# Delta rule on one Trainium2 core: the triangular mask on the query products alone, and the decay exponentials in a buffer of their own

## The chip, the cores and the metric

The kernel runs on one core of a Trainium2 chip. The metric is the device time of one execution in microseconds (us); lower is better. The time before is the median of three runs. The profile is of one further execution, which has a time of its own, and sums are made against that one. The engines are named as in the profile: PE is the matrix engine (PEld its weight loads), DVE the vector engine, ACT the engine of activation functions, POOL the general engine, SP the engine that issues most transfers.

## What is computed

One layer of a hybrid encoder serves two groups of tokens with shared weights: a prompt of 512 tokens and a sample of 64. Its first half is a gated delta rule of 4 heads, each 128 wide, beside a differential attention; then follow an attention over a memory and a feed-forward block. The change touches the delta rule alone. Cut to what matters, its reference is:

```python
G = jnp.cumsum(gc, axis=-1)
diff = G[..., :, None] - G[..., None, :]
gam = jnp.where(tril, jnp.exp(jnp.where(tril, diff, 0.0)), 0.0)
kk = jnp.einsum('nbhid,nbhjd->nbhij', kc, kc)
a_sys = jnp.where(strict, bc[..., :, None] * kk * gam, 0.0) + jnp.eye(C)
u = triangular_solve(a_sys, bc[..., None] * vc, ...)
w = triangular_solve(a_sys, (bc * jnp.exp(G))[..., None] * kc, ...)
qk = jnp.einsum('nbhid,nbhjd->nbhij', qc, kc) * gam
qg = qc * jnp.exp(G)[..., None]

def step(S, xs):
    vn = u_c - w_c @ S
    o = qg_c @ S + qk_c @ vn
    S = S * gl_c + kd_c.T @ vn
```

So the decay factors `gam` enter twice: into the system that is solved (strictly triangular) and into the products of queries and keys (triangular). The plain exponentials `exp(G)` scale keys and queries where they meet the running state `S`.

## The kernel before, in words

The activations lie transposed, features on partitions, and most of the work is projections: 128 output columns at a time are loaded from the weights by SP (L148, L153), split into a high and a low part by ACT and DVE (L157, L158), and multiplied on PE in three products that add up in a bank of PSUM (`project`, L165). In the profile these matmuls are `pr<-u,wh` and `pr<-u,wl`.

The delta rule works on five chunks: four of 128 prompt tokens (c = 0 to 3) and one of 64 sample tokens (c = 4). `gdn_prep` (L566) makes what a chunk needs without the state, and `gdn_scan` (L683) carries the state `S` through it. The program order is prep 0, prep 1, the projection of the gate z, scan 0, prep 2, scan 1, prep 3, scan 2, prep 4, scan 3, scan 4. The time in which each engine takes its instructions is not written out by hand here: a planner with a model of costs orders each engine's queue at compile time, by readiness and program order, and it mixes the projections in between. On the chip each engine then takes its queue strictly in that order and waits by semaphores. So a change of dependencies can also change the order of unrelated instructions.

In `gdn_prep`, in order: keys and queries are turned (L576, L584), squared and summed for their norms (L580 to L588), and POOL takes the reciprocal roots (`rpow`, L204, called at L589). The cumulated decay is spread over rows by PE into the bank `bg` (L596). DVE subtracts (L599) into the buffer `Y`, ACT takes the exponential (L602), and POOL multiplies by the triangular mask `triu` (L603): this is `gam`. PE makes the products of keys (L606), DVE multiplies them with `gam` and a factor into `At` (L609). PE makes the products of keys and queries (L614), DVE multiplies them with `gam` into `KQ` (L616). The values are turned (L623) and scaled into `vb` (L625). For c > 0 ACT takes the exponential of `bg` into the buffer `eg` (L628), and POOL multiplies keys and queries by it (L629, L630). Then the inverse of the system is built up by doubling: `masked` (L632) picks from `At` the entries of one level by the table `lev`, whose lower triangle is zero (L541), into a buffer `B`; PE, ACT and DVE alternate (L643 to L679) until the inverse is `X`.

Two kinds of buffers matter. The banks of PSUM named g0 and g1 belong to even and odd chunks and there is one of each, so that all products of one chunk's prep pass through one bank, each after the readers of the one before. The SBUF buffers `B0` and `B1` have two copies each, and `sq`, `eg` and `B` of a chunk share them. The buffer `aT` has two copies too and is used by the two attentions later (L861, L1000).

`gdn_scan` ends with a norm of its output: ACT squares (L718), DVE sums (L719 to L721), POOL takes the root (L722, in the profile L204), DVE scales (L723, L724). Beside the delta rule the memory is normed at L516: ACT squares (L222), DVE and POOL take the root (L227, L204), DVE scales (L232), PE turns it.

Of the kernel before, what the change touches and what calls it, by code (L numbers as in the profile page):

```python
# [10 lines left out]
AF = mybir.ActivationFunctionType  # L11
ALU = mybir.AluOpType
# [22 lines left out]
def hybrid_layer_kernel(  # L35
# [10 lines left out]
    V, A, G = nc.vector, nc.scalar, nc.gpsimd  # L46
# [28 lines left out]
    def nm(s):  # L75
        uid[0] += 1
        return f"{s}_{uid[0]}"
# [10 lines left out]
    def small(tag, shape, bufs=None):  # L88
        tag = SHARED.get(tag, tag)
        bufs = 1 if tag in ("vn", "on", "S") or tag[:-1] in ("At", "Dt", "Y") else 2  # L90
        return sp.tile(shape, F32, tag=tag, name=nm(tag), bufs=bufs)

    def tiny(shape, tag="tiny", bufs=16):
        return tp.tile(shape, F32, tag=tag, name=nm(tag), bufs=bufs)

    def bank(tag="ba"):
        return ps.tile([P, 512], F32, tag=tag, name=nm(tag), bufs=BANKS[tag])

    def const(shape, name, dt=F32):
        return cp.tile(shape, dt, tag=name, name=name)  # L100
# [40 lines left out]
    triu = const([P, P], "triu")  # L141
# [259 lines left out]
    for typ in (1, 0, 2):  # L401
        cT[typ] = (e5[:, 1], e2[:, 1], e2[:, 0])[typ]
        for h in range(H):
# [7 lines left out]
            n = SOFF + DEC  # L411
# [135 lines left out]
    def v4(ap, n):  # L547
        return ap.rearrange("p (h n) -> p h n", h=4)[:, :, :n]

    def sb(tag, bufs=2):  # L550
        return small(tag, [P, 4, P], bufs)
# [14 lines left out]
    def gdn_prep(c, c0, n):  # L566
        L = slice(c0, c0 + n)

        def st(tag):
            return sb(dict(gam="Y", sq="B", eg="B").get(tag, tag) + str(c % 2))  # L570

        r8 = tiny([P, 8], "tg")
        s8 = tiny([P, 8], "tg")
# [3 lines left out]
        kd = sb("kd")  # L577
        V.tensor_tensor(kd[:n], v4(bk, P)[:n], kdc[:n, c, :].unsqueeze(2).to_broadcast([n, 4, P]), ALU.mult)
        sq = st("sq")
        A.activation(sq[:n], v4(bk, P)[:n], AF.Square)  # L580
        V.tensor_reduce(s8[:n, 0:4], sq[:n], AX.X, ALU.add)
        bq = bank(f"g{c % 2}")
        for h in range(H):
            tr(bq[:n, h * P : (h + 1) * P], cq[:, h, L])  # L584
        sq2 = st("sq")
        A.activation(sq2[:n], v4(bq, P)[:n], AF.Square)
        V.tensor_reduce(s8[:n, 4:8], sq2[:n], AX.X, ALU.add)
# [6 lines left out]
        bg = bank(f"g{c % 2}")  # L594
        for h in range(H):
            mm(bg[:, h * P : h * P + n], bc(gg[:n, c, h : h + 1], [n, P]), triu[:n, :n])  # L596
        gam = st("gam")
        for h in range(H):
            V.tensor_scalar(  # L599
                gam[:n, h, :n], bg[:n, h * P : h * P + n], Gc[:n, c, h : h + 1], 0.0, ALU.subtract, ALU.min  # L600
            )
        A.activation(gam[:n, :, :n], gam[:n, :, :n], AF.Exp)  # L602
        G.tensor_tensor(gam[:n, :, :n], gam[:n, :, :n], triu[:n, :n].unsqueeze(1).to_broadcast([n, 4, n]), ALU.mult)  # L603
        bkk = bank(f"g{c % 2}")
        for h in range(H):
            mm(bkk[:n, h * P : h * P + n], ck[:, h, L], ck[:, h, L])  # L606
# [7 lines left out]
            mm(bkq[:n, h * P : h * P + n], ck[:, h, L], cq[:, h, L])  # L614
        KQ = sb("KQ")
        V.tensor_tensor(KQ[:n, :, :n], v4(bkq, n)[:n], gam[:n, :, :n], ALU.mult)  # L616
        nk, rq2 = tiny([P, 4], "tg"), tiny([P, 4], "tg")
        V.tensor_tensor(nk[:n], s8[:n, 0:4], r8[:n, 0:4], ALU.mult)
        V.tensor_scalar(r8[:n, 4:8], r8[:n, 4:8], P ** -0.5, None, ALU.mult)
# [4 lines left out]
        vb = sb("vb")  # L624
        V.tensor_tensor(vb[:n], v4(bv, P)[:n], nk[:n].unsqueeze(2).to_broadcast([n, 4, P]), ALU.mult)  # L625
        if c > 0:
            eg = st("eg")
            A.activation(eg[:, :, :n], v4(bg, n), AF.Exp)  # L628
            G.tensor_tensor(ck[:, :, L], ck[:, :, L], eg[:, :, :n], ALU.mult)  # L629
            G.tensor_tensor(cq[:, :, L], cq[:, :, L], eg[:, :, :n], ALU.mult)  # L630

        def masked(lv):  # L632
            B = st("B")
            V.scalar_tensor_tensor(  # L634
                B[:n, :, :n], lev[:n, :n].unsqueeze(1).to_broadcast([n, 4, n]), float(lv), At[:n, :, :n],
                ALU.is_equal, ALU.mult,
            )
            return B
# [3 lines left out]
        B = masked(1)  # L642
# [6 lines left out]
        while lv < n:  # L649
            Y = st("Y")  # L650
            by = bank(f"g{c % 2}")
            if lv < 64:
                B = masked(lv)
# [76 lines left out]

    S = None
    prepared = [gdn_prep(*chunks[0][:2], chunks[0][3])]
    for c, c0, t0, n in chunks:
        if c < 4:
            prepared.append(gdn_prep(*chunks[c + 1][:2], chunks[c + 1][3]))
        else:
            nc.sync.dma_start(o_gdn_p[0, 0].rearrange("h k v -> k h v"), S)
            S = sb("S")
            nc.sync.dma_start(S, state_gdn[0, 0].rearrange("h k v -> k h v"))
        if c == 0:  # L740
            project_z()
        S = gdn_scan(c, c0, t0, n, prepared[c], S)
# [256 lines left out]
    for h in range(H):  # L999
# [14 lines left out]
        for t, (q0, _) in enumerate(QT):  # L1014
            t0, n = TT[t]
# [181 lines left out]
```

## Time and profile before

| what | us |
|---|---|
| median of 3 runs (lowest to highest) | 1063.34 (1062.84 to 1063.38) |
| the profiled execution, its own time | 1061.57 |
| its span, first to last instruction | 1059.5 |
| PE busy of the span | 1034.8 |
| DVE, ACT, POOL busy | 671.5, 432.6, 73.8 |

All times in the traces count from the span's start. A row of the timeline gives start, duration, engine, line, operation and `out<-in`, and, in brackets, the idle time of that engine just before and what ended it. A row of windows gives, for a stretch, its length, the busy time of PE, PEld, DVE, ACT and POOL with the number of instructions, the granted PE clock as a share of full speed, the share of the transfer engines and GB/s. Since the three products of a projection are the bulk of the work, PE is busy nearly always; a busy PE can still run at half its clock, which the column of the clock shows.

### The profile page before, as it was taken

What the parts mean: (1) busy time and instruction counts of PE and PEld (TensorE: products, weight loads), DVE (VectorE), ACT (ScalarE), POOL (GpSimd) and SP (SyncE); (2) the same over time, 40 slices, a digit from 0 to 9 for tenths busy, and PEclk for the clock granted to TensorE, in tenths of its full rate; (3) what the DMA queues carried; (4) which work ended last, traced back from release to release, by engine and by line L of the source; (5) the groups of instructions that cost most, each with busy time, mean ns of one, the idle gap of its engine ahead of it and who ended that gap; (6) DMA issues with size and microseconds to landing.
All of it is one profiled execution on the core that took longest, in us unless ns stands there. A gap on an engine that the chain in (4) does not pass through costs nothing.

```text
span 1059.5 us, 16941 instructions
## 1 busy us (share of the span) xinstructions
PE 1034.8 (98%) x6574; PEld 929.9 (88%) x6574; DVE 671.5 (63%) x1471; ACT 432.6 (41%) x897; POOL 73.8 (7%) x126
## 2 busy tenths in 40 slices
PE   8999899999999999999999999999999999999997
PEld 6999898898788877999887799999999999999996
DVE  6767684756467575564555666666666666666674
ACT  6644754333265665343333443323232323222344
POOL 4411120311000000000000000000000000000000
PEclk9999999999999999999999999999999999999998
DMA  7332310100132255524211122132414141323312
GB/s 212 116 120 78 114 41 21 42 1 22 54 88 63 89 179 198 166 80 140 60 41 40 57 83 63 58 100 60 116 47 124 44 119 50 110 59 109 91 51 90
DMA packets 139442, 89.96 MB, mean 85 GB/s; under 512 B 5522, under 2 KB 130576, under 8 KB 138852
## 3 DMA queue, kind: packets, MB, share of 16 engines
q1 hardware_dynamic: 138996, 88.24, 28.0%
q8 instruction: 52, 0.85, 0.3%
q10 hardware_dynamic: 368, 0.66, 0.2%
q14 instruction: 26, 0.21, 0.1%
HBM read 79.14 MB, written 9.74 MB: 84 GB/s over the span
## 4 chain that ended last, share of the span: by engine, by line
PE 90%; issue 4%; DVE 2%; ACT 2%; POOL 1%; DMA 0%; POOLq 0%; ACTq 0%; DVEq 0%
PE pr L103 70%; PE g L103 10%; PE gs L103 3%; PE ba L109 3%; PE ba L103 2%; PE g L109 2%; POOL tg L204 1%; POOL tiny L204 0%; PE pr L109 0%; PE gs L109 0%; ACT wh L157 0%; ACT u L1109 0%; ACT Y L656 0%; POOL u L630 0%; DVE on L724 0%
## 5 line engine op out<-in xcount | busy, mean ns | idle before, releaser
L103 PE MATMUL pr<-u,wh 128*128 128x512 f32 (+1 forms) x2664 | 699.5, 343 | 1.2 <-DVE u L288 0.9
L103 PEld LDWEIGHTS pr<-u,wh 128*128 128x128 f32 x2664 | 456.5, 188 | 37.8 <-issue 1.7
L103 PE MATMUL pr<-u,wl 128*128 128x256 f32 (+1 forms) x1776 | 484.7, 299 | 0.0
L103 PEld LDWEIGHTS pr<-u,wl 128*128 128x128 f32 x1776 | 328.4, 189 | 8.0 <-DVE wl L355 0.3
L157 ACT CAST wh<-raw 128x1024 fp32r<-128x1024 f32 (+1 forms) x153 | 136.5, 892 | 231.2 <-PE pr L103 212.4
L158 DVE TENSOR_TENSOR wl<-raw,wh 128x1024 fp32r<-128x1024 f32 (+1 forms) x153 | 157.4, 1029 | 61.3 <-ACT wh L157 59.5
L943 DVE TENSOR_TENSOR u<-u,pr 128x256 f32<-128x256 f32 (+1 forms) x160 | 72.3, 452 | 62.8 <-PE pr L103 60.2
L204 POOL TENSOR_TENSOR tiny<-tiny,nhalf 128x1 f32<-128x1 f32 (+4 forms) x11 | 10.1, 918 | 664.1 <-DVE tiny L1127 409.3
L197 ACT CAST u<-p 128x256 fp32r<-128x256 f32 x64 | 27.8, 435 | 51.8 <-DVE p L1064 51.8
L103 PE MATMUL pr<-wh,u 128*128 128x512 f32 x128 | 42.6, 405 | 0.0
L198 DVE TENSOR_TENSOR u<-p,u 128x256 fp32r<-128x256 f32 x64 | 29.2, 457 | 15.2 <-ACT u L197 15.2
L190 ACT COPY p<-pr 128x256 f32<-128x256 f32 (+1 forms) x44 | 16.4, 373 | 51.3 <-PE pr L103 51.3
L191 DVE TENSOR_TENSOR p<-pr,p 128x256 f32<-128x256 f32 (+1 forms) x44 | 18.6, 422 | 26.9 <-ACT p L190 26.9
L945 DVE TENSOR_TENSOR u<-u,pr 128x256 f32<-128x256 f32 x80 | 33.6, 420 | 2.4
L1063 DVE TENSOR_TENSOR p<-pr,rB 128x320 f32<-128x320 f32 x32 | 15.7, 492 | 25.7 <-PE pr L103 25.7
L415 DVE SCALAR_TENSOR_TENSOR p<-p,gcol,p 128x579 f32<-128x579 f32 x33 | 27.1, 821 | 6.4 <-ACT p L413 5.9
L1064 DVE SCALAR_TENSOR_TENSOR p<-p 128x256 f32<-128x256 f32 x64 | 29.3, 458 | 2.2
L665 ACT COPY X<-g 128x512 f32<-128x512 f32 (+1 forms) x24 | 13.2, 550 | 42.6 <-PE g L109 42.5
L200 ACT ACTIVATE u<-u,gcol 128x256 fp32r<-128x256 f32 (+1 forms) x32 | 17.0, 534 | 31.1 <-DVE u L945 31.1
L103 PE MATMUL g<-u,qz 128*128 128x256 f32 (+4 forms) x96 | 29.5, 411 | 0.0
L103 PEld LDWEIGHTS pr<-wh,u 128*128 128x128 f32 x128 | 23.6, 188 | 4.5 <-issue 0.2
L634 DVE SCALAR_TENSOR_TENSOR B<-lev,At 128x512 f32<-128x512 f32 (+1 forms) x30 | 20.7, 696 | 10.6 <-PE g L103 8.8
(317 smaller groups left out, 1211.8 us busy)
## 6 DMA issues: line engine op xcount, KB each, us to landing
raw<-in_w_ff_dram SPq DMA_DIRECT2D x32, 512.0 KB
raw<-in_w_ff_dram SPq DMA_DIRECT2D x64, 256.0 KB
raw<-in_w_in_dram SPq DMA_DIRECT2D x28, 512.0 KB
raw<-in_w_mem_k_dram SPq DMA_DIRECT2D x8, 512.0 KB
raw<-in_w_mem_v_dram SPq DMA_DIRECT2D x8, 512.0 KB
raw<-in_w_out_dram SPq DMA_DIRECT2D x8, 512.0 KB
raw<-in_w_mem_q_dram SPq DMA_DIRECT2D x8, 512.0 KB
raw<-in_w_mem_o_dram SPq DMA_DIRECT2D x8, 512.0 KB
```

The costliest lines, as they stand in the source:

```text
L103: i = nc.tensor.matmul(out, lhsT, rhs, start=start, stop=stop)
L109: i = nc.tensor.transpose(out, in_, ident[:n, :n])
L157: A.copy(wh, raw)
L158: V.tensor_tensor(wl, raw, wh.bitcast(F32), ALU.subtract)
L197: A.copy(h, src)
L198: V.tensor_tensor(lo, src, h.bitcast(F32), ALU.subtract)
L204: G.tensor_tensor(out, in_, bc(nhalf[: in_.shape[0], 0:1], list(in_.shape)), ALU.pow)
L415: V.scalar_tensor_tensor(yv[:, :n], cb[:, i : i + n], cwt[:, m, i : i + 1], yv[:, :n], ALU.mult, ALU.add)
L634: V.scalar_tensor_tensor(B[:n, :, :n], lev[:n, :n].unsqueeze(1).to_broadcast([n, 4, n]), float(lv), At[:n, :, :n], ALU.is_equal, ALU.mult,)
L943: V.tensor_tensor(hm, hm, b, ALU.add)
L945: V.tensor_tensor(hm, hm, more, ALU.add)
L1064: V.scalar_tensor_tensor(f, f, 0.0, f, ALU.max, ALU.mult)
```

## The change

The mask moves from `gam` to `KQ`: POOL no longer multiplies `gam` by `triu` between the exponential and its two readers, but multiplies `KQ` by it after DVE has made it. `At` is then made from an unmasked `gam`; its lower triangle is never read, since `lev` is zero there and the last level reads the upper right quarter alone. The number and the sizes of the POOL instructions stay the same, five on 128x512 (64x256 for the last chunk). The exponential into `eg` moves up to stand right behind that of `gam`, and `eg` takes the buffer `aT` in place of a copy of `B0` or `B1`. No matmul, no transfer and no activation is added or taken away.

```diff
         def st(tag):
-            return sb(dict(gam="Y", sq="B", eg="B").get(tag, tag) + str(c % 2))
+            return sb(dict(gam="Y", sq="B").get(tag, tag) + str(c % 2))
...
         A.activation(gam[:n, :, :n], gam[:n, :, :n], AF.Exp)
-        G.tensor_tensor(gam[:n, :, :n], gam[:n, :, :n], triu[:n, :n].unsqueeze(1).to_broadcast([n, 4, n]), ALU.mult)
+        if c > 0:
+            eg = sb("aT")
+            A.activation(eg[:, :, :n], v4(bg, n), AF.Exp)
         bkk = bank(f"g{c % 2}")
...
         KQ = sb("KQ")
         V.tensor_tensor(KQ[:n, :, :n], v4(bkq, n)[:n], gam[:n, :, :n], ALU.mult)
+        G.tensor_tensor(KQ[:n, :, :n], KQ[:n, :, :n], triu[:n, :n].unsqueeze(1).to_broadcast([n, 4, n]), ALU.mult)
...
         if c > 0:
-            eg = st("eg")
-            A.activation(eg[:, :, :n], v4(bg, n), AF.Exp)
             G.tensor_tensor(ck[:, :, L], ck[:, :, L], eg[:, :, :n], ALU.mult)
             G.tensor_tensor(cq[:, :, L], cq[:, :, L], eg[:, :, :n], ALU.mult)
```

## The prediction

> **What bounds the kernel now.** I read the page first, then the busy time by stretches, then PE's waits in the stretch of the delta rule, and last the order of instructions around each wait that the change can touch.
>
> ```profile
> span 1059.5 us, 16941 instructions
> PE 1034.8 (98%) x6574; PEld 929.9 (88%) x6574; DVE 671.5 (63%) x1471; ACT 432.6 (41%) x897; POOL 73.8 (7%) x126
> 104.00:290.00 186.00, 179.93 (x1364) 159.43 (x1363) 120.92 (x286) 78.93 (x139) 32.54 (x28) 0.99 0.14 41
> 290.00:1059.50 769.50, 755.92 (x4606) 681.41 (x4604) 479.35 (x1064) 295.00 (x646) 9.36 (x11) 1.00 0.30 89
> ```
>
> PE is busy for 98% of the span. The delta rule lies between 104 and 290 us, and even there projections fill PE: it idles 186.00 − 179.93 = 6.1 us. The change adds no work to PE and takes none away, so it can only move PE's idle time and the time that PE spends at a low clock. These are PE's waits in that stretch (line, what it waited for, us in total, times, longest):
>
> ```profile
> PE g L103 <- DVE At L609: 2.1, 1, 2.1
> PE g L109 <- DVE vb L625: 1.5, 1, 1.5
> PE gs L103 <- DVE on L724: 1.4, 2, 0.8
> ```
>
> The first two, 3.6 of 6.1 us, hang on code that the change edits. The first is in chunk 0:
>
> ```profile
> 125.85 0.63 ACT L602 ACTIVATE Y<-Y 128x512 f32<-128x512 f32 x1
> 127.36 1.65 POOL L204 TENSOR_TENSOR tg<-tg,nhalf 128x8 f32<-128x8 f32 x1 [2.08 <-DVE tg L588]
> 127.78 0.14 DVE L592 TENSOR_TENSOR tg<-tg,beta 128x4 f32<-128x4 f32 x1
> 128.97 1.28 POOL L603 TENSOR_TENSOR Y<-Y,triu 128x512 f32<-128x512 f32 x1
> 129.12 0.28 PE L103 MATMUL pr<-u,wl 128*128 128x256 f32 x1
> 130.28 1.12 DVE L609 SCALAR_TENSOR_TENSOR At<-g,tg,Y 128x128 f32<-128x128 f32 x4 [2.36 <-POOL Y L603]
> 131.46 1.55 PE L103 MATMUL g<-u,u 128*128 128x128 f32 x8 [2.06 <-DVE At L609]
> 128.50:131.46 2.96, 0.90 (x6) 0.53 (x4) 1.18 (x5) 2.10 (x3) 1.75 (x2) 1.00 0.10 40
> 131.46:131.90 0.44, 0.44 (x4) 0.44 (x4) 0.44 (x2) 0.20 (x1) 0.00 (x0) 1.00 0.00 0
> 131.90:135.30 3.40, 3.40 (x15) 3.01 (x14) 2.37 (x5) 3.37 (x5) 2.65 (x2) 0.53 0.18 35
> ```
>
> The exponential is ready at 126.48. The mask starts only at 128.97, because POOL first takes a root for chunk 1 (L204). So `At` starts at 130.28, and the key-query products, which need `At` to free their bank, start at 131.46, after PE has stood still for 2.06 us. Right behind that the granted clock falls to 0.53 for 3.40 us, which costs 3.40 × (1 − 0.53) = 1.6 us more.
>
> **The change part by part**, as differences to the profiled execution.
>
> *The mask leaves the path to `At`, chunk 0.* `At` then needs the exponential (126.48) and what stands before it in DVE's queue, which ends at 127.92. It can start at 127.95, 2.3 us earlier; the products could start at about 129.1, and PE's last projection before them ends at 129.40. The wait of 2.06 goes: **−2.06** (bounds 0 and −2.06, as the order in DVE's queue may change). Without the wait I expect no fall of the clock: **−1.6** (bounds 0 and −1.6).
>
> [...]
>
> *What is late next.* Behind those products PE turns the normed memory. These rows set when it can:
>
> ```profile
> 130.68 0.19 ACT L222 ACTIVATION_READ_ACCUMULATOR u<-u 128x1 f32 x1
> 132.18 1.22 DVE L158 TENSOR_TENSOR wl<-raw,wh 128x1024 fp32r<-128x1024 f32 x1
> 132.41 2.14 POOL L603 TENSOR_TENSOR Y<-Y,triu 128x512 f32<-128x512 f32 x1 [2.16 <-ACT Y L602]
> 133.32 0.14 DVE L227 TENSOR_SCALAR tiny<-tiny 128x1 f32<-128x1 f32 x1
> 133.38 0.68 DVE L616 TENSOR_TENSOR KQ<-g,Y 128x512 f32<-128x512 f32 x1
> 134.50 0.56 POOL L204 TENSOR_TENSOR tiny<-tiny,nhalf 128x1 f32<-128x1 f32 x1
> 135.09 1.28 DVE L232 SCALAR_TENSOR_TENSOR u<-u,tiny,gB 128x1024 f32<-128x1024 f32 x1 [1.03 <-POOL tiny L204]
> 137.11 1.03 PE L109 MATMUL ba<-ident,u 128*128 128x128 f32 x8
> ```
>
> From 131.46 to the turn at 137.11 PE has 5.65 us, at full clock 5.65 − 1.6 = 4.05; starting at 129.40 it arrives at 133.45. With DVE's order shifted by 2.3 us, L158 ends at 131.1, L227 at 131.2, the root (0.56, no longer behind chunk 1's mask) at about 132.1, L232 at about 133.5 and the turn can start at about 133.7: **+0.3**. If the new mask of chunk 0's `KQ` (`KQ` done at about 131.9, 1.28 for the mask) gets ahead of that root on POOL, the root ends at 133.8, L232 at 135.2, and PE waits about 2.0 us. Bounds 0 and +2.0. I take 0.3, since L227 stands ahead of `KQ` in DVE's queue.
>
> *Chunk 2.* Its wait of 1.45 us hangs on `eg` in the buffers `B0`:
>
> ```profile
> 195.40 1.45 POOL L629 TENSOR_TENSOR u<-u,B 128x512 f32<-128x512 f32 x1 [4.91 <-PE g L103]
> 195.62 0.68 DVE L616 TENSOR_TENSOR KQ<-g,Y 128x512 f32<-128x512 f32 x1
> 196.82 1.74 POOL L630 TENSOR_TENSOR u<-u,B 128x512 f32<-128x512 f32 x1
> 198.52 1.01 POOL L204 TENSOR_TENSOR tg<-tg,nhalf 128x4 f32<-128x4 f32 x1
> 198.59 0.69 DVE L634 SCALAR_TENSOR_TENSOR B<-lev,At 128x512 f32<-128x512 f32 x1 [1.19 <-POOL u L630]
> 199.94 0.66 PE L109 MATMUL g<-ident,X 128*128 128x128 f32 x4 [1.45 <-DVE vb L625]
> 200.27 0.68 DVE L724 TENSOR_TENSOR on<-gs,tg 128x512 f32<-128x512 f32 x1
> 201.12 0.38 PE L103 MATMUL gs<-vn,kd 128*128 128x128 f32 x2
> 221.86 0.69 DVE L634 SCALAR_TENSOR_TENSOR B<-lev,At 128x512 f32<-128x512 f32 x1 [0.38 <-POOL u L630]
> ```
>
> A `B` needs the copy that `eg` holds until L630 has read it, and `vb` stands behind that `B`. With `eg` in `aT` the 1.19 us go, `vb` and PE's turn come 1.2 earlier: −1.2. Against it: the mask of `KQ` (1.28) now stands on POOL among L629 and L630, ahead of the scan's root at 198.52, which waits in their queue already. Then the root ends at 200.8, L724 runs from about 201.3 to 202.0, and the state products, at 201.12 before, start at about 202.1: +1.0, with PE, which arrives 1.2 earlier, waiting about 2.2. That is more than the 2.06 which the fall of the clock followed, so the bound is +1.0 + 1.6 = +2.6. I take the middle of −1.2 and +1.0, rounded: **0**.
>
> *Chunks 1, 3, 4.* No wait of PE stands behind L603 there; the mask of `KQ` is read by the scan, many us later. What could be saved is the 0.38 us that a `B` of chunk 3 waits for L630 (the last row above), and no PE wait follows it. I take 0, bounds 0 and −0.4.
>
> *Locking between POOL and DVE.* A short instruction on DVE, of a kind that takes 0.15 us elsewhere (the last row), shows what POOL's mask can do to DVE:
>
> ```profile
> 189.21 1.28 POOL L603 TENSOR_TENSOR Y<-Y,triu 128x512 f32<-128x512 f32 x1 [0.65 <-ACT Y L602]
> 189.34 1.16 DVE L620 TENSOR_TENSOR tg<-tg 128x4 f32<-128x4 f32 x1
> L720 DVE TENSOR_TENSOR tg<-tg,tg 128x4 f32<-128x4 f32 x1 | 0.2, 152 | 0.0
> ```
>
> L620 ends at 190.50, with the mask (190.49). The mask keeps its five instructions, so such stalls (about 1.0 us each) move with it, from the time behind `gam` to that behind `KQ`, where `B` and `X` follow on DVE. PE has projections to do meanwhile: I take 0, bounds −1.0 and +1.0.
>
> *The exponential that moves.* In the trace it already stands right behind the other:
>
> ```profile
> 188.50 0.63 ACT L602 ACTIVATE Y<-Y 128x512 f32<-128x512 f32 x1 [1.91 <-DVE Y L599]
> 189.16 0.60 ACT L628 ACTIVATE B<-g 128x512 f32<-128x512 f32 x1
> ```
>
> So this part alone is worth 0 on ACT; its effect is that of the buffer. If the order did change, ACT has 186.00 − 78.93 = 107 us free in the stretch.
>
> *The order of the queues.* The planner will order all engines anew from chunk 0 on. No row prices this. What is left of PE's idle time is 6.1 − 2.06 − 1.45 = 2.6 us; a new order can at best save that and I let it cost as much: 0, bounds ±2.6.
>
> **Sum:** −2.06 − 1.6 + 0.3 + 0 = −3.4 us. The profiled execution took 1061.57 us: its span of 1059.5 and 2.07 around it. So 1058.2 on its scale. The median of the runs, 1063.34, is 1.77 above that execution; on its scale **1059.9**. After 290 us projections follow each other and the transfers use 0.30 of the engines, so I expect the gain to be kept to the end.
>
> **The rivals.**
>
> *The clock falls anyway (0.07).* If the fall at 131.90 isn't bound to the wait, only 2.06 − 0.3 = 1.8 is saved: 1061.5. For it: the waits of 1.45 us and less are not followed by a fall, so one instance is all there is. [...] Against: it starts 0.44 us after the wait.
>
> *The mask is paid back in chunk 2 (0.17).* Chunk 0 gains 3.4, the root of scan 1 comes late and PE waits long enough for a fall of the clock: −3.4 + 2.6 = −0.8, 1062.5. For it: the root's input was ready before L629 began and it still stood behind L630. Against: the planner sees the mask and may put the root first.
>
> *Slower: POOL's queue is the new bound (0.16).* The mask of `KQ` stands ahead of a root in both places. In chunk 0 PE then waits 2.0 us at the memory's turn with a fall of the clock, and the gain there is about 0; chunk 2 costs 2.6: 1065.9. It decides from the point where the mask is queued ahead of both roots. For it: `KQ` and L227 are neighbours on DVE. Against: L227 is the earlier one.
>
> *Both gains come (0.08).* The root is queued ahead of the mask in chunk 2: −3.4 − 1.2 = −4.6, 1058.7.
>
> That the change does not do what it says holds for its second half: the exponential does not move on ACT. This is in the sum.
>
> **How the numbers follow.** The forecast, 1059.9, has 0.52; with the bounds of the new order its own range is 1057.3 to 1062.5. A measurement of this kernel can tell 0.2%, 2.1 us, from no change. Faster by more than that: most of the forecast (0.47), both gains (0.08), a part of the clock case (0.02): 0.57. Within: 0.04 of the forecast, 0.05 of the clock case, 0.15 of chunk 2's: 0.24. Slower: the rest, 0.19. The range 1057.0 to 1065.0 leaves out most of the slower case (0.13) and some 0.06 below.
>
> **What would show it.** In chunk 0 `At` starts at about 128 us, PE's wait of 2.06 is gone, and no stretch of the delta rule has a clock near 0.5. In chunk 2 no `B` waits for L630. If PE's waits for L724 or for L232 grow past 2 us, the mask is paid back on POOL. If the sum of PE's idle time between 104 and 290 stays at 6 us without such a wait, the new order took it. A later stage that waits where it did not would make the forecast wrong.

## The result and the profile after

The changed kernel takes 1067.07 us (median of 5 runs, 1066.0 to 1069.21) beside 1062.91 us before (5 runs, 1062.84 to 1063.38): a ratio of 1.0046, 95% interval 1.0036 to 1.0057. It is slower by about 4 us (0.4%), outside the predicted range and above the slowest of the prediction's rivals (1065.9). The profiled execution took 1066.0 us.

The page of the changed kernel (span, then busy time of each engine), and below it two stretches of its windows (columns as before):

```profile
span 1064.3 us, 16941 instructions
PE 1036.1 (97%) x6574; PEld 930.1 (87%) x6574; DVE 676.0 (64%) x1471; ACT 435.6 (41%) x899; POOL 75.1 (7%) x126
```

```profile
104.00:290.00 186.00, 178.14 (x1357) 157.24 (x1356) 122.37 (x277) 80.97 (x141) 33.28 (x27) 1.00 0.15 44
290.00:1064.30 774.30, 758.65 (x4613) 683.76 (x4613) 482.58 (x1072) 295.87 (x647) 10.05 (x12) 0.99 0.29 88
587.20:590.60 3.40, 2.94 (x7) 2.17 (x8) 1.11 (x4) 0.27 (x1) 0.00 (x0) 0.50 0.02 5
```

The engines are about as busy as before, so nothing was added but waiting. PE's idle time in the delta rule did not shrink by 3.3 us; it grew from 6.1 to 186.00 − 178.14 = 7.9 us. The clock there is now whole, but 3.40 us at half clock stand at 587, far behind, and behind 290 us PE idles 774.30 − 758.65 = 15.7 us, 2.1 more than before. PE's waits over the whole run that are new or that the prediction spoke of:

```profile
PE g L109 <- DVE vb L628: 3.2, 2, 1.8
PE gs L103 <- DVE on L725: 1.8, 3, 0.8
PE ba L109 <- DVE u L794: 1.3, 1, 1.3
PE g L103 <- ACT p L853: 1.0, 2, 0.8
PE ba L109 <- DVE u L232: 0.8, 1, 0.8
```

The wait for `At` is gone. In its place PE waits in smaller portions: for DVE, and, in a later stage that the change doesn't touch, for an exponential of the attention heads on ACT (L853). Neither the wait for L725 (L724 before) nor that for L232 has grown past 2 us, the sign that the prediction named for its rivals; the largest, for `vb`, was not among these signs. Three places of the timeline show why. Chunk 0:

```profile
127.68 1.12 DVE L611 SCALAR_TENSOR_TENSOR At<-g,tg,Y 128x128 f32<-128x128 f32 x4
129.00 1.05 PE L103 MATMUL g<-u,u 128*128 128x128 f32 x8
132.19 2.38 DVE L232 SCALAR_TENSOR_TENSOR u<-u,tiny,gB 128x1024 f32<-128x1024 f32 x1
132.20 1.29 POOL L619 TENSOR_TENSOR KQ<-KQ,triu 128x512 f32<-128x512 f32 x1
134.62 1.09 PE L109 MATMUL ba<-ident,u 128*128 128x128 f32 x8 [0.84 <-DVE u L232]
```

`At` starts at 127.68 and the products at 129.00, as forecast. But the mask of `KQ` (L619) runs from 132.20 to 133.49, and DVE's scaling of the memory (L232) takes 2.38 us where it took 1.28 before. Where the text below says that one of these two engines holds or locks the other, it means such a longer row beside a row of the other engine, and no more than that. Chunk 1:

```profile
148.63 1.41 POOL L630 TENSOR_TENSOR u<-u,aT 128x512 f32<-128x512 f32 x1 [8.95 <-PE g L103]
149.41 4.54 DVE L635 SCALAR_TENSOR_TENSOR B<-lev,At 128x512 f32<-128x512 f32 x3
150.00 1.73 POOL L631 TENSOR_TENSOR u<-u,aT 128x512 f32<-128x512 f32 x1
151.69 1.71 POOL L619 TENSOR_TENSOR KQ<-KQ,triu 128x512 f32<-128x512 f32 x1
153.88 0.68 DVE L628 TENSOR_TENSOR vb<-g,tg 128x512 f32<-128x512 f32 x1
154.61 0.66 PE L109 MATMUL g<-ident,X 128*128 128x128 f32 x4 [1.82 <-DVE vb L628]
```

Three products of POOL now stand back to back. Beside them three `B` take 4.54 us (one alone takes 0.69), `vb` stands behind them, and PE waits 1.82. Chunk 2:

```profile
198.17 1.75 POOL L631 TENSOR_TENSOR u<-u,aT 128x512 f32<-128x512 f32 x1
199.88 2.32 POOL L619 TENSOR_TENSOR KQ<-KQ,triu 128x512 f32<-128x512 f32 x1
201.73 0.66 PE L109 MATMUL g<-ident,X 128*128 128x128 f32 x4 [1.43 <-DVE vb L628]
202.16 1.45 POOL L204 TENSOR_TENSOR tg<-tg,nhalf 128x4 f32<-128x4 f32 x1
204.26 0.33 PE L109 MATMUL ba<-ident,u 128*128 128x128 f32 x1 [1.29 <-DVE u L794]
```

The mask stands between L631 and the scan's root (L204), which ends at 203.61; before it ended at 199.53. PE waits 1.43 for `vb` and then 1.29 for a copy that stands behind the norm's instructions on DVE (L794).

To see where the time goes, one measure is used below. Each matmul of the trace is priced at what its shape takes in a dense row of them, the prices are summed, and two kernels are compared at equal sums: the **lag** is how many us later (or, below zero, earlier) than the profiled execution of before a kernel has done the same work of PE. It is worked out from PE's rows, to some 0.3 us. The numbers at the head are places on the clock of before; 140 lies behind chunk 0, 156 behind chunk 1's wait, 200 ahead of chunk 2's inverse, 205 behind it, 260 ahead of the attention heads, 410 behind them, 600 behind the attention over the memory.

| kernel | 140 | 156 | 200 | 205 | 260 | 410 | 600 |
|---|---|---|---|---|---|---|---|
| changed kernel | −2.3 | −0.8 | −2.4 | +0.3 | +0.8 | +3.5 | +5.0 |
| no mask at all (e1) | −3.8 | −3.3 | −4.9 | −3.5 | −3.0 | −0.4 | −0.4 |
| mask early, beside the products (e2) | −2.5 | −2.0 | −3.6 | −2.2 | −1.8 | +0.8 | +2.4 |
| before in the new order of PE (e8) | +0.7 | +1.5 | −0.1 | +1.0 | +1.0 | +3.6 | +5.4 |
| the change, old orders held (e12) | −2.7 | −2.0 | −2.2 | +0.5 | +0.8 | +0.9 | +2.6 |
| mask folded, old orders held (e11) | −3.3 | −3.2 | −3.5 | −3.2 | −2.9 | −2.9 | −2.3 |

The lags tell places, not medians: e1's profiled execution, for one, is its fastest (1060.67). The first row is the whole story: 2.3 us gained in chunk 0, then losses in chunk 1, in chunk 2 (2.7), in the attention heads (2.7), where no code was edited, and at a fall of the clock (1.5).

### The profile page after: what moved, and what is told of

Read it like the earlier page. It is cut to its first block, busy times and chain, and to the rows that moved or that the text cites. A ratio compares the mean times of both kernels' runs of the same rounds, so it can differ in the third digit from the quotient of the medians.

```text
span 1064.3 us, 16941 instructions
## 1 busy us (share of the span) xinstructions
PE 1036.1 (97%) x6574; PEld 930.1 (87%) x6574; DVE 676.0 (64%) x1471; ACT 435.6 (41%) x899; POOL 75.1 (7%) x126
## 4 chain that ended last, share of the span: by engine, by line
PE 73%; issue 4%; DVE 1%; ACT 1%; POOL 1%; POOLq 0%; ACTq 0%
PE pr L103 59%; PE g L103 6%; PE gs L103 2%; PE ba L109 2%; PE ba L103 2%; PE g L109 1%; POOL tg L204 0%; ACT p L853 0%; ACT u L1110 0%; DVE B L635 0%; POOL tiny L204 0%; DVE on L725 0%; DVE u L944 0%; PE gs L109 0%; POOL ta L204 0%
## 5 line engine op out<-in xcount | busy, mean ns | idle before, releaser
L158 DVE TENSOR_TENSOR wl<-raw,wh 128x1024 fp32r<-128x1024 f32 (+1 forms) x153 | 158.2, 1034 | 63.2 <-ACT wh L157 61.4
L204 POOL TENSOR_TENSOR tiny<-tiny,nhalf 128x1 f32<-128x1 f32 (+4 forms) x11 | 10.5, 951 | 663.7 <-DVE tiny L1128 409.2
L1064 DVE TENSOR_TENSOR p<-pr,rB 128x320 f32<-128x320 f32 x32 | 15.7, 492 | 25.8 <-PE pr L103 25.8
```

The source lines that it names most:

```text
L158: V.tensor_tensor(wl, raw, wh.bitcast(F32), ALU.subtract)
```

## The experiments

All ratios are to the kernel before, run beside on the same chip, with a 95% interval.

The theory at the outset: the mask on POOL pays the gain back, by standing ahead of a root and by locking DVE. Rival: the planner's new order does it, whatever the mask costs. A second rival: `eg`'s new buffer. The move of the exponential by itself was not run; of the change's second half only the buffer was tested.

**e1, no mask.** Leaves out the mask: `KQ` keeps entries above its diagonal. PE, ACT and DVE keep the order of the changed kernel.

```diff
-        G.tensor_tensor(KQ[:n, :, :n], KQ[:n, :, :n], triu[:n, :n].unsqueeze(1).to_broadcast([n, 4, n]), ALU.mult)
```

> The changed kernel with the mask of KQ left out altogether (so the products of queries and keys keep their upper triangle); every engine's order but POOL's is that of the changed kernel. Theory P (POOL's pile: the mask stands in a row with the two products by eg, holds DVE and delays a root): chunk 1's 2.0 us and chunk 2's 2.7 us go, so 1067.1 - 4.7 = about 1062.4. Theory O (the new order of the queues costs the time, not the mask): the time stays near 1067, within 1 us. Theory C (the clock's fall in a late stage differs by chance from kernel to kernel): either, plus or minus 1.7.

1062.59 us (1060.67 to 1062.86, 11 runs), 0.9995 [0.9986, 1.0003]. So the mask on POOL costs 1067.07 − 1062.59 = 4.5 us, but what is left is no gain: this kernel has gained 3.8 us behind chunk 0 and 3.0 by 260 us, and has lost it again by 410. In chunk 1 (timeline) the three `B` now take 3.47 us and PE waits 0.74:

```profile
147.95 3.47 DVE L634 SCALAR_TENSOR_TENSOR B<-lev,At 128x512 f32<-128x512 f32 x3
148.54 1.73 POOL L630 TENSOR_TENSOR u<-u,aT 128x512 f32<-128x512 f32 x1
152.07 0.66 PE L109 MATMUL g<-ident,X 128*128 128x128 f32 x4 [0.74 <-DVE vb L627]
```

**e2, the mask early and beside.** The five POOL instructions stay; they write the masked factors into `KQ`'s buffer right behind the exponential, off the path to `At`.

```diff
+        KQ = sb("KQ")
+        G.tensor_tensor(KQ[:n, :, :n], gam[:n, :, :n], triu[:n, :n].unsqueeze(1).to_broadcast([n, 4, n]), ALU.mult)
...
-        V.tensor_tensor(KQ[:n, :, :n], v4(bkq, n)[:n], gam[:n, :, :n], ALU.mult)
-        G.tensor_tensor(KQ[:n, :, :n], KQ[:n, :, :n], triu[:n, :n].unsqueeze(1).to_broadcast([n, 4, n]), ALU.mult)
+        V.tensor_tensor(KQ[:n, :, :n], v4(bkq, n)[:n], KQ[:n, :, :n], ALU.mult)
```

> The mask stays on POOL but is made early, from gam into the buffer of KQ, beside the path to At; KQ is then the product with it. PE's and ACT's orders are those of the changed kernel. P: the mask is done before the products by eg start, the pile of chunks 1 and 2 is gone: about 1062.5, like e1. O: near 1067. If it lies between e1 and the changed kernel, the mask's lock on DVE costs also where it is early.

1063.47 us (1062.04 to 1063.67, 11), 0.9999 [0.999, 1.0008]. Against e1 the lag is 1.3 larger behind chunk 0, where `KQ` now waits for the mask (it takes 3.40 us there, beside DVE's work, and 1.28 to 1.29 in chunks 1 and 2), and no larger anywhere after it up to 560 us. So it isn't POOL's work as such that costs in chunks 1 and 2, but its place: behind `KQ` it runs beside DVE's `B`, and in these two chunks it does not ahead of the products.

**e3, the buffer alone**, and **e4, the mask alone**: the two halves of the change.

```diff
-            eg = st("eg")
+            eg = sb("aT")
```

> Before, with eg in aT and nothing else changed; the planner's order of PE differs from before in 378 rows. P: no pile; chunk 2's wait of 1.45 goes, so 1062.9 - 1.2 = about 1061.7. O: the new order alone moves the time by up to 3 us either way, slower if new orders tend to be worse.

```diff
-        G.tensor_tensor(gam[:n, :, :n], gam[:n, :, :n], triu[:n, :n].unsqueeze(1).to_broadcast([n, 4, n]), ALU.mult)
...
         V.tensor_tensor(KQ[:n, :, :n], v4(bkq, n)[:n], gam[:n, :, :n], ALU.mult)
+        G.tensor_tensor(KQ[:n, :, :n], KQ[:n, :, :n], triu[:n, :n].unsqueeze(1).to_broadcast([n, 4, n]), ALU.mult)
```

> Before, with the mask moved to KQ and eg left in its buffer and place. P: the pile is there, and the B that waits for eg's reader as well: as slow as the changed kernel or up to 1.2 slower, 1067 to 1068. O: not tied to the changed kernel's time, anything from 1060 to 1067.

e3: 1066.3 us (1064.73 to 1067.07, 6), 1.0032 [1.002, 1.0044]. e4: 1066.06 us (1065.08 to 1066.8, 6), 1.0031 [1.0019, 1.0042]. Either half alone is slower, which the theory did not expect of e3. Its buffer takes no work and no wait on to PE's path; but it also gives PE a third order, neither that of before nor that of the changed kernel, and 2.1 us of its lag arise in the attention heads (+0.2 at 260 us, +2.3 at 410). Halves that come with orders of their own can't be added up, so the order became the main suspect. In e4's profile 1.6 us of the lag stand ahead of the delta rule, at 104 us; behind that it loses some 1.7 us in chunk 1 and 3.2 in chunk 2, where the changed kernel loses 1.6 and 2.7.

**e5, the mask folded away.** No POOL instruction: the bound of DVE's subtraction becomes a table with 0 where the mask is 1 and −1e30 where it is 0, so that the exponential yields the zeros. PE and ACT keep the changed kernel's order.

```diff
+        neg = const([P, P], "neg")
+        V.tensor_scalar(neg, triu, 1e30, -1e30, ALU.mult, ALU.add)
...
-            V.tensor_scalar(
-                gam[:n, h, :n], bg[:n, h * P : h * P + n], Gc[:n, c, h : h + 1], 0.0, ALU.subtract, ALU.min
+            V.scalar_tensor_tensor(
+                gam[:n, h, :n], bg[:n, h * P : h * P + n], Gc[:n, c, h : h + 1], neg[:n, :n], ALU.subtract, ALU.min
...
-        G.tensor_tensor(KQ[:n, :, :n], KQ[:n, :, :n], triu[:n, :n].unsqueeze(1).to_broadcast([n, 4, n]), ALU.mult)
```

> The changed kernel without POOL's mask: the mask is folded into DVE's subtraction, which takes the minimum with a constant that is 0 in the triangle and -1e30 above it in place of the minimum with 0, so that the exponential gives 0 there. PE's, ACT's and POOL's orders are those of e1. M (POOL's mask behind KQ costs about 4.5 us, the arithmetic is nothing): as e1, 1062.6. Rival: the subtraction, now with two operands, gets slower or is held by POOL: 1063 to 1065.

1062.1 us (1061.76 to 1063.52, 11), 0.9998 [0.9989, 1.0006]. As e1: the whole computation without the mask on POOL, and still no gain. Something takes about 3 us from all of these kernels.

**The heads.** The orders of PE and of ACT are the same in the changed kernel, e1, e2 and e5, and e1, e2 and the changed kernel lose the same 2.6 to 2.7 us between 260 and 410 us. The stretch 260 to 425 us of the windows, in before, e1 and the changed kernel:

```profile
260.00:425.00 165.00, 162.96 (x977) 133.03 (x976) 101.80 (x280) 89.22 (x251) 7.48 (x9) 1.00 0.35 109
```

```profile
260.00:425.00 165.00, 161.49 (x966) 131.16 (x966) 101.33 (x280) 88.21 (x250) 7.18 (x9) 1.00 0.35 110
```

```profile
260.00:425.00 165.00, 161.49 (x982) 131.16 (x980) 101.69 (x283) 89.05 (x252) 7.96 (x11) 1.00 0.33 103
```

e1 and the changed kernel have PE and PEld less busy than before by the same 1.47 and 1.87 us (the lag is larger, 2.6 to 2.7; an estimate from the two is that some 1.2 us of it lie in time that counts as busy). The waits of weight loads for the heads' exponentials (in us, times, longest) agree, first before, then the changed kernel:

```profile
PEld g L103 <- ACT p L852: 1.8, 8, 0.4
```

```profile
PEld g L103 <- ACT p L853: 3.2, 9, 1.1
```

To test the order by itself, the queues of one kernel were fixed in the listed order of another, by dependencies that hold at compile time only and put no wait into the program:

```diff
+    for first, then in zip(queue, queue[1:]):
+        tc.add_manual_dep(then, first.name, mybir.DependencyInfo(mybir.DependencyClass.NoSync, mybir.DependencyReason.DATA), reason="order")
```

**e6** is e5, **e7** the changed kernel, both with PE's queue held in the order of before; **e8** is before with PE's queue in the order of the changed kernel.

> e5 with PE's queue fixed to the order that it has in the kernel before (all 5986 matmuls). O (the new order of PE costs 2.6 us in the attention heads, 260 to 425 us, whatever the mask does): 1062.6 - 2.6 = 1060.0. Rival A (the loss in the heads comes from eg in aT or from the other queues): as e5. The wait for At in chunk 0 should be gone in either, with the half clock behind it.

> The changed kernel, mask of KQ on POOL as it is, with PE's queue fixed to the order of the kernel before. O and M together: the mask's 4.5 stay, the heads' 2.6 go: 1067.1 - 2.6 = 1064.5. Rival A: 1067.

> The kernel before, unchanged, with PE's queue fixed to the order that it has in the changed kernel. O: 1062.9 + 2.6 = about 1065.5, the wait for At in chunk 0 and its half clock stay. Rival A: 1062.9, as before.

e6: 1068.96 us (1067.79 to 1069.32, 5), 1.0055 [1.0043, 1.0068]. e7: 1072.47 us (1071.46 to 1072.86, 5), 1.0089 [1.0075, 1.0102]. e8: 1065.07 us (1064.72 to 1066.88, 8), 1.0025 [1.0014, 1.0035].

e8 answers: before, with its code unchanged and PE's queue in the new order, loses the same 2.6 us in the heads (lag +1.0 to +3.6), with the same long waits (below). It doesn't show PE's order alone: the planner, to which ACT and DVE were left, fitted them to PE's queue, and by the traces both have the order of the changed kernel from 261 us on. In e6 and e7, with PE in the order of before, ACT and DVE have that of before in the heads. So PE's order brings the others along, and which of the three queues costs the time is not divided.

```profile
PEld g L103 <- ACT p L852: 2.9, 8, 1.1
```

e6 and e7 missed, since holding one engine alone brought in a wait of its own. The new orders of ACT and DVE put chunk 1's decay factors and its `eg` late, while PE's old order wants `eg` early. In e6:

```profile
PE g L103 <- ACT aT L607: 5.8, 1, 5.8
```

Their heads lose nothing (e6's lag is 6.2 at 260 and at 410), but that wait buries the gain. So the next four hold PE, ACT and DVE, all in the order of before, and leave only POOL and SP to the planner.

**e9** is e3 under these orders, **e10** and **e11** are before with the mask folded, with `eg` in `B` and in `aT`, **e12** is the change itself, with the exponential at its old place in the program (ACT's order is held anyway). The table of e10 and e11 is made at the start by POOL instead of DVE:

```diff
+        G.memset(neg, 0.0)
+        G.affine_select(out=neg, in_=neg, pattern=[[1, P]], compare_op=ALU.is_ge, fill=-1e30, base=0, channel_multiplier=-1)
```

> Before with eg in aT, and PE's, ACT's and DVE's queues all fixed to the orders that they have in the kernel before. Theory F (each part is worth what its wait shows once the orders are held): the 1.2 us that a B waits for eg's reader go: 1062.9 - 1.2 = 1061.7; at least not slower than 1062.9. Rival (the buffer aT itself is what made e3 slow): 1066.

> Before without POOL's mask (folded into DVE's subtraction, as in e5), eg in B as before, all three queues fixed to the orders of before. F: the wait of 2.06 in chunk 0 and the half clock behind it go, 1062.9 - 3.7 = 1059.2. Rival (the old orders have a wait behind that one, as e6 met with PE's queue alone): 1061 or more.

> e10 with eg in aT. F: both gains, 1062.9 - 3.7 - 1.2 = 1058.0, the fastest of all; if the state's root takes back the second, 1059.2. Rival: as in e10, 1061 or more.

> The change itself (mask of KQ on POOL, eg in aT), all three queues fixed to the orders of before. M (POOL's mask behind KQ costs 1.5, 1.0 and 1.3 us in chunks 0, 1 and 2, as the changed kernel against e1): e11 plus 3.8, about 1062. Rival (the pile was harmful only with the new orders): as e11, 1058 to 1059.

| kernel, orders of before held | us (range, runs) | ratio to before |
|---|---|---|
| e9, buffer alone | 1063.37 (1061.7 to 1064.49, 11) | 1.0005 [0.9997, 1.0014] |
| e10, mask folded | 1059.71 (1057.99 to 1061.33, 9) | 0.9975 [0.9965, 0.9985] |
| e11, mask folded, buffer | 1058.93 (1058.55 to 1060.78, 5) | 0.9968 [0.9955, 0.998] |
| e12, the change | 1063.89 (1062.53 to 1065.84, 11) | 1.0013 [1.0004, 1.0021] |

e11 beats both kernels. Its chunk 0 (timeline) shows what the prediction described, with L232 at 1.28:

```profile
128.06 1.12 DVE L611 SCALAR_TENSOR_TENSOR At<-g,tg,Y 128x128 f32<-128x128 f32 x4
129.45 1.05 PE L103 MATMUL g<-u,u 128*128 128x128 f32 x8
132.03 1.28 DVE L232 SCALAR_TENSOR_TENSOR u<-u,tiny,gB 128x1024 f32<-128x1024 f32 x1
133.70 1.03 PE L109 MATMUL ba<-ident,u 128*128 128x128 f32 x8
```

e9 was expected to gain and did not. A `B` no longer waits for L630's release of a buffer, but in chunk 2 it is held all the same:

```profile
196.21 2.89 DVE L634 SCALAR_TENSOR_TENSOR B<-lev,At 128x512 f32<-128x512 f32 x2
196.82 1.74 POOL L630 TENSOR_TENSOR u<-u,aT 128x512 f32<-128x512 f32 x1
199.76 0.66 PE L109 MATMUL g<-ident,X 128*128 128x128 f32 x4 [1.30 <-DVE vb L625]
```

Two `B` take 2.89 us instead of 2 × 0.69, and PE waits 1.30 where it waited 1.45: the wait for a buffer became a lock by the same instruction.

e12 against e11 is the mask on POOL, 1063.89 − 1058.93 = 5.0 us (the fold changes DVE's subtraction besides, but one of them takes 0.34 us in either), of which chunk 2 takes most (e12's lag goes from −2.2 to +0.5, e11's from −3.5 to −3.2) and a fall of the clock at 586 us another 1.7. In chunk 2 the root goes first and the mask second, and the lock shows by itself:

```profile
196.45 1.45 POOL L204 TENSOR_TENSOR tg<-tg,nhalf 128x4 f32<-128x4 f32 x1
197.88 1.26 POOL L616 TENSOR_TENSOR KQ<-KQ,triu 128x512 f32<-128x512 f32 x1
197.94 1.22 DVE L723 TENSOR_TENSOR tg<-tg,tg 128x4 f32<-128x4 f32 x1 [0.30 <-POOL tg L204]
199.62 0.59 PE L109 MATMUL ba<-ident,u 128*128 128x128 f32 x3 [1.15 <-DVE u L793]
```

L723, on 4 columns, begins 0.06 us behind the mask and ends 0.02 us behind it. Then PE waits 1.15, its second wait there (1.27 for `vb` at 197.69), and the windows give half a clock for the next 3.40 us:

```profile
200.00:203.40 3.40, 3.40 (x17) 3.31 (x16) 1.89 (x3) 1.08 (x3) 0.16 (x1) 0.50 0.28 60
```

## Why the prediction was wrong, step by step

- *Chunk 0, −2.06 and −1.6:* right. Without the mask on POOL the gain stands (e11: −3.3, e1: −3.8 at 140 us), and no fall of the clock follows, so the rival "the clock falls anyway" was wrong. By the medians e10 and e11 are 2.8 and 3.6 us faster than before (1062.51, run beside them): this term, kept to the end. The half clock of before begins at 132.08 us, not at 131.90 (the stretch that the prediction showed takes in 0.17 us at full clock), so its cost is 3.41 × 0.5 = 1.7; that changes little.
- *The memory's turn, +0.3:* too small. L227 did go ahead of `KQ`, and the root of the memory was not delayed by the mask. But the mask held L232 from 1.28 to 2.38 us. The changed kernel stands at −2.3 at 140 us, 1.5 short of e1; PE's wait of 0.84 is the part of it that one row shows.
- *Locking between POOL and DVE, 0:* the first step that failed. The prediction saw the lock in a row (L620 at 1.16), saw that it moves to where `B` and `X` follow, and took 0 because PE has projections to do. But `vb` and the products that free the bank stand behind the `B` on DVE, and no projection filled the wait: in chunk 1 of the changed kernel PE runs nothing from 152.79 to 154.61 us, and the projections that stand behind the waiting turn come after it, from 155.02. The rows show what the stalls amount to: L232 took 2.38 us beside the mask and 1.28 without it, L723 1.22 (e12) and 0.16, three `B` 4.54 and one alone 0.69.
- *Chunks 1, 3, 4, 0:* failed for chunk 1. In before PE waits for nothing there (no wait between 140 and 180 us); in the changed kernel the mask came to stand beside the `B`, and PE waits for the `vb` behind them. Lag 1.6 us in the changed kernel (−2.4 at 150 to −0.8), 0.5 in e1.
- *Chunk 2, 0:* 1.1 as a net (lag −0.8 at 156 to +0.3 at 205), inside its bounds, and made of two parts like the two ends of the bound: 1.6 gained by 200 us, as `B` went early, 2.7 lost behind the late mask and root. That the gain was the buffer's is not supported: e8, with before's code in the new order, gains 1.6 there too, and e9, with the buffer in the old order, nothing.
- *The order of the queues, 0, bounds ±2.6:* the second step that failed, at its bound. The loss of 2.6 us stands in the heads, behind the edited code, and e8 shows it without the change. It was bounded from the idle time of the delta rule, which is not where it fell: the order was changed in the stage behind it as well. A later stage that waits where it did not was the last of the signs that the prediction named, and it came.
- *The clock:* the fall went from 132 to 587 us and took 1.5 us there. The prediction looked for falls in the delta rule only. In part this is chance, since whether a fall comes at 587 differs between kernels with the same wait of 2.0 us there (last section). Four of the changed kernel's five runs have a mean clock of 0.994, the profiled one 0.996; a fall is worth 3.41 × 0.5 / 1064 = 0.0016 of it, so by this estimate the other four have one fall more than the lags show.

The sum by the lags, in order of time: −2.3 + 1.6 − 1.6 + 2.7 + 0.5 (205 to 260 us, not divided further) + 2.7 + 1.5 = +5.1 us, beside a span longer by 4.8. The rival "the mask is paid back in chunk 2" was right in its place and, with the lock, in its mechanism, but alone it did not decide; the rival that POOL's queue delays both roots was wrong in chunk 0. The change with the order taken out is e12: 1.4 us slower than before, a gain of 3.6 (e11) and 5.0 for the mask.

What stays open: how the 2.7 us of chunk 2 in the changed kernel divide between the late root and the lock (e12 shows that the lock alone is enough for a wait of 1.15); why the heads' exponentials come later in the new order, beyond the fact that they do in each of the five kernels that have it; which of the queues' new orders, PE's, ACT's or DVE's, costs the time there; and whether what the last section reads from two profiles about the falls of the clock holds when nothing but the place of the grid is changed.

## What to carry to other kernels

When work is moved off a path on to another engine, look not only for its queue but for who runs beside it there: a cost that was a plain wait at the old place (PE's 2.06 us for `At`) can be a lock on a third engine at the new one (L232 at 2.38 us for 1.28), so fold such work into an instruction that exists (here a bound in a subtraction) rather than moving it. Where a planner orders the queues, a change of dependencies comes with a new order for stages that it doesn't touch; hold the order of all engines, not of one, before the change itself is judged. And a wait for a buffer is worth nothing until it is known what the same instruction does next (in e9 1.30 us of PE's wait were left of 1.45).

## What the runs showed of the hardware

- **POOL and DVE held each other in these rows.** A POOL product of 1.26 us held a DVE instruction of 0.16 us for 1.22 us (e12, L723). The other way round, the mask, 1.26 to 1.29 us where it comes first, took 2.32 us in chunk 2 of the changed kernel, where DVE's L158 had begun 0.02 us ahead of it:

```profile
199.86 1.22 DVE L158 TENSOR_TENSOR wl<-raw,wh 128x1024 fp32r<-128x1024 f32 x1
199.88 2.32 POOL L619 TENSOR_TENSOR KQ<-KQ,triu 128x512 f32<-128x512 f32 x1
```

One more row of the changed kernel: L722 (128x4) takes 1.26 us beside L631, from 198.69 us to 199.95, as L631 ends at 199.92; the same instruction takes 0.17 in e12, where POOL is idle. Not every row beside POOL is longer: `vb` (L628) takes 0.68 us at 201.00, while the mask runs, and 0.68 at 153.88, where POOL is idle. What sets the two kinds apart is not shown.

- **The same wait with and without a fall of the clock.** In the attention over the memory PE waits 2.0 us for the same value in before, the changed kernel, e1, e2, e11 and e12. In the changed kernel, e2 and e12 the stretch 580 to 592 us has a clock of 0.86, in before, e1 and e11 of 1.00. First before (waits, then the stretch), then e12:

```profile
PE ba L109 <- DVE p L1026: 2.7, 3, 2.0
```

```profile
580.00:592.00 12.00, 8.92 (x39) 5.43 (x39) 4.94 (x17) 3.55 (x13) 0.00 (x0) 1.00 0.01 1
```

```profile
PE ba L109 <- DVE p L1026: 2.6, 2, 2.0
```

```profile
580.00:592.00 12.00, 8.70 (x30) 5.05 (x29) 4.57 (x17) 2.93 (x10) 0.00 (x0) 0.86 0.01 1
```

So here a wait of 2 us isn't enough for a fall, and by e12 at 200, with 1.27 and 1.15, no single wait of 2 us is needed. The fall lasts 3.413 us in before and 3.414 in the changed kernel, and one costs about 1.5 (the lag at 587) to 1.7 (3.41 × 0.5). The clock records of these two profiles fit steps of 3.4133 us: the stretch at full clock up to the fall is 119.466 us long in before, 35 steps, and 573.438 in the changed kernel, 168; the one from there to the half clock at the end of the profile is 918.185, 269 steps, and 467.626, 137. This grid begins at another place in each, 12.61 us behind the span's start in before and 13.75 in the changed kernel.
- **What a fall follows.** Cut along this grid, the stretches at full clock ahead of 1040 us have 299 steps in before and as many in the changed kernel. In each, one step is followed by half a clock, and it is the one in which PE is busy least: for 0.40 of it in before, 0.39 in the changed kernel. Of the other 596 steps the least busy has 0.55, in either kernel. Before's step runs from 128.66 to 132.07 us; with 0.40 of it busy, PE was not idle for the whole of the step ahead of that fall. In the attention over the memory the wait of 2.0 us has a shorter one ahead of it (0.58 us, ended 3.25 us earlier). In the changed kernel one step (583.77 to 587.18) holds the short wait and 1.5 us of the long one; it is busy for 0.39, and a fall follows. In before the step with most of the long wait (582.63 to 586.04) holds no part of the short one; it is busy for 0.55, and none does. So in these two profiles the fall goes with how much of PE's waiting lies in one step; two falls don't show a limit. This is read from the profiles, with a busy time whose ends are modelled; no run changes the grid's place alone, and the half clock at the end of each profile, where the matmuls stop, is left aside. The author's guess, which no run shows, is that the place of the grid also makes the spread of one kernel: e5's 11 runs lie either at 1061.8 to 1062.2 us, with a mean clock of 0.997 to 0.998, or at 1063.1 to 1063.5 us, with 0.996 to 0.997.
